# The scheduler takes account of the SBUF port that VectorE and GpSimd share, and the mixers' second weight parts are computed on VectorE

## The chip, the cores and the metric

The kernel runs on one core of a Trainium2 chip. Its engines are TensorE (PE in the profile, its weight loads PEld), VectorE (DVE), ScalarE (ACT), GpSimd (POOL) and SyncE (SP, which here only issues DMAs). The metric is the device time of the whole program in microseconds; lower is better.

## The reference

Four layers over 512 tokens (256 of context, then 256 latent), each with 1024 channels:

```
for l in range(DEPTH):                                  # 4 layers, all in float32
    hg, rw, gt = split(modulate(rms_norm(x)) @ w_in[l]) # 1024 x 6528
    o_hg = hgrn2_branch(hg)     # gated linear recurrence, both directions, 4 heads of 128
    o_rw = rwkv7_branch(rw)     # delta-rule state update, both directions, 8 heads of 64
    m = sigmoid(g_hg) * (o_hg @ proj_a) + sigmoid(g_rw) * (o_rw @ proj_b)
    x = x + gate * rms_norm(m @ w_out)
    x = x + gate2 * rms_norm((silu(gt) * up) @ ffn_w2)  # gt, up = h @ ffn_w1, hidden size 2816
```

Scale, shift and gate of each sub-layer come from a small modulation, silu(c) @ ada_w (1024 x 6144 a layer). In the last layer only the 256 latent tokens are read.

## The kernel before, in words

**Tiles and stages.** Channels lie on the 128 partitions, tokens on the free axis (512 of them). Each layer has two stages. In the *mixers* the input projection feeds four head pairs of RWKV-7 and four heads of HGRN2. In *merge and FFN* come proj_a, proj_b, w_out, the norms and SwiGLU, with the modulation of the next sub-layers computed beside them on VectorE (`ada_pair`: four multiply-adds of 128x512 for each loaded tile `hq` or `PB`).

**Split weights.** Every product is made of three matmuls on rounded numbers. `load_split` loads 128x512 of weights (`wr`), ScalarE rounds them (`wh`, or a place lent by another tile), and another engine subtracts to get the second part (`wl`): `lo = raw - hi`. I call such a subtraction a *second part*. A layer has 270 of them: 102 for the mixers' projection, 16 for proj_a and proj_b, 16 for w_out, 136 for the FFN. Their engine is set by `LO`, with an entry for the mixers and one for the rest in the first three layers, then the same for the last layer: 0 is GpSimd, 1 is either engine, as the scheduler finds them free.

**The mixers' chains.** For an RWKV pair, `rw_solve` inverts triangular matrices with 60 small steps on VectorE (tiles `XS` and `S`), each reading what the one before wrote. `rw_chain` then walks eight chunks: matmuls into `c_ps`, `S0P = S * pcs` on GpSimd, and VectorE's updates of `UV` and `S` that read `S0P`. An HGRN2 head has seven levels, with multiplications `hX`, `hY` on VectorE and running sums `SF`, `PF`, `PB`, `SB` on GpSimd. The projection's matmuls (`p_ps`) fill TensorE between these.

**What sets the order.** All instructions are first written down (`Plan.add`) with a cost from a table (`cost`) and then list-scheduled (`schedule`): each engine takes, of what could start, what the longest chain of work hangs on. The hardware then runs each engine's list in order. The tables `PAR`, `BIAS` and `LOOK` steer that schedule; they are the same before and after.

Of the kernel before, what the change touches and what calls it, by code (L numbers as in the profile page):

```python
# [16 lines left out]
P = 128  # L17
D = 1024
NK = 8
T = 512  # L20
# [41 lines left out]
LO = (1, 0, 1, 1)  # L62
# [9 lines left out]
MAXLOOK = 200  # L72
WINDOW, COLD = 4096 / 1.2, (0.39, 0.87)
# [10 lines left out]
class Node:  # L84
    """One instruction, or several of an engine in a row, with what it waits for."""
# [3 lines left out]
    def __init__(self, engs, calls, preds, costs, load, kind):  # L89
        self.engs, self.calls, self.preds, self.costs, self.load, self.kind = engs, calls, preds, costs, load, kind  # L90


class Plan:
    """Takes down the kernel's instructions, and emits them in the order of a list schedule: each engine runs, of what
    could start, what the longest chain of work hangs on."""
# [10 lines left out]
    def lo(self, i):  # L106
        """The engine of the weights' second parts."""
        return self.any if LO[i] else self.pool

    def tile(self, pool, shape, dt, tag, bufs, name):  # L110
        """A tile; one of a tag takes the place of the one that its tag gave out bufs tiles before."""
# [12 lines left out]
    def region(a):  # L124
        """Partitions and elements that an access pattern spans."""
# [13 lines left out]
    def together(self):  # L139
        """The instructions recorded in this context, all of one engine, stay one after another."""  # L140
        @contextmanager
        def group():
            self.gang = -1
            yield
            self.gang = None
        return group()

    def add(self, engs, name, args, kw):
# [23 lines left out]
        preds.discard(n)  # L172
        b = 4
# [8 lines left out]
        else:  # L182
# [3 lines left out]
            self.nodes.append(Node(engs, [(name, args, kw)], preds, costs, load, self.kind))  # L186
# [8 lines left out]
    @staticmethod  # L195
    def cost(eng, name, out, args, kw):
        """Nanoseconds that an instruction holds its engine."""
# [8 lines left out]
        if eng == "pe":  # L206
# [6 lines left out]
            if args[1].dtype == F32R:  # L213
                return max(n / 2.4, m / 1.2) + 2.5
# [6 lines left out]
        if eng == "vec":  # L221
            if name == "memset":
                return n * 1.05
            two = name in ("tensor_scalar", "tensor_copy") and not psum
# [3 lines left out]
        if name == "tensor_scalar":  # L228
            if ptr:
                return 686.0  # L230
# [10 lines left out]
    def schedule(self):  # L241
# [26 lines left out]
        tail = 1e9  # L268

# [8 lines left out]
        while len(order) < N:  # L278
# [26 lines left out]
            _, i = heapq.heappop(ready[e])  # L305
            x = nodes[i]
            on[i] = e
            c = x.costs[x.engs.index(e)]
# [43 lines left out]
def body(ctx, tc, xT, cc, ada_w, w_in, rw_lo, rw_g2, proj_a, proj_b, w_out, ffn_w1, ffn_w2,  # L352
# [122 lines left out]
    def load_split(src, k0, nk, c0, ncol, place=None):  # L475
        """Weight rows k0*128.. and columns c0.. as its rounded part and the rest."""
# [24 lines left out]
    def psum2(w, src, hi, lo, rg=slice(0, T), tag="s"):  # L501
        """PSUM tile with w^T src for w of zeros and ones, src going in two parts."""
# [7 lines left out]
    def spots(tile):  # L510
        """Places for the split weights of one output tile in [P, 4, T]."""
# [7 lines left out]
    def proj(src, nk, c0, xh, xl, t0, place=None):  # L519
        """PSUM tile with W[:, c0:c0+128]^T x for tokens t0.., with a place for the weights stream by stream."""  # L520
# [24 lines left out]
    def norms(xs, t0, post=None, pre=None):  # L545
        """x += G * rms_norm(y), and then h = rms_norm(x) * A + B per channel and stream, split in two parts."""
# [79 lines left out]
    def ada_put(pm, b, n, ps):  # L626
        """Sums of n blocks of columns from b on, each stream's in 128 / 2 n rows, put channel-major in md."""
# [12 lines left out]
    def ada_first(l, pm):  # L640
        """The first four blocks of 512 columns of silu(c) @ ada_w[l], each in a quarter of the rows."""
# [14 lines left out]
    def ada_pair(l, pm, b):  # L656
        """Blocks b and b + 1, the products summed over the rows of each partition first."""
# [22 lines left out]
    def ada_finish(pm, i):  # L680
        """Scale, shift and gate of sub-layer i // 3 with the norm weights in."""
# [31 lines left out]
    def sigm(o, src, nb, t):  # L713
        """o = sigmoid(src - nb) by exp and ln; t is all of o."""
# [5 lines left out]
    def shifted(ps, j, lmu, t0, tag):  # L720
        """pf = p + mu (shift(p) - p) of projection tile j."""
# [20 lines left out]
    def layer(l, pm, xs, xd, hh, hl):  # L742
# [772 lines left out]
```

## Time and profile before

| | us |
|---|---|
| median of 3 runs | 4484.12 (4477.95 to 4488.85) |
| span of the profiled execution | 4491.0 |
| VectorE busy in it | 3314.2 (74%) |
| TensorE busy in it | 4151.3 (92%) |
| GpSimd busy in it | 2318.9 (52%) |

The profiled execution's span is 6.9 us (0.15%) over the median and 2.2 us over the slowest of the three runs; no work is shown outside the span. Shares of busy time are averages over stages; TensorE's matmuls overlap each other in the records, so its share says little by itself.

### The profile page before, as it was taken

Reading aid. Unit: us, or ns where it says so; the run is one execution under the profiler, and the core shown is the slowest. Engines: PE = TensorE matmul, PEld = TensorE weight load, DVE = VectorE, ACT = ScalarE, POOL = GpSimd, SP = SyncE. Lnnn points to the kernel's source line nnn. Section 1 sums busy time; section 2 is a strip of 40 time slices with the busy share of each in tenths; the row PEclk is TensorE's granted clock in tenths of the full one; section 3 lists DMA queues with packets and bytes.
Section 4 is the critical chain, followed back from the end, with each engine's and each line's share of the span. In section 5 each row is a group of like instructions: output and inputs, shape, how many; then the busy total and the mean of one; then the engine's idle time right before and its main releaser. Section 6 shows DMA issues by size and latency. Waiting matters only on the chain. (4 is left out here: it accounts for less than half of the span.)

```text
span 4491.0 us, 72501 instructions
## 1 busy us (share of the span) xinstructions
PE 4151.3 (92%) x26290; PEld 3248.2 (72%) x26290; DVE 3314.2 (74%) x5772; ACT 2161.3 (48%) x4458; POOL 2318.9 (52%) x2121
## 2 busy tenths in 40 slices
PE   7999998899999999989999999999899989888998
PEld 5676776677777767778777676677777766667888
DVE  5988878977388898676627988876754487887665
ACT  4554653433255565534434554554433354554564
POOL 2464654465445456454654554554555535455542
PEclk8998899999998998899999998899999988887999
DMA  4211127455421111354433211116444421111555
GB/s 151 59 46 36 51 88 227 140 166 158 134 73 57 49 44 46 125 173 125 139 114 122 63 49 41 46 56 205 122 146 124 137 67 43 41 44 39 159 151 162
DMA packets 661415, 451.08 MB, mean 100 GB/s; under 512 B 28224, under 2 KB 584256, under 8 KB 661056
## 3 DMA queue, kind: packets, MB, share of 16 engines
q1 hardware_dynamic: 661056, 446.44, 33.1%
q8 instruction: 207, 3.39, 0.3%
q14 instruction: 152, 1.25, 0.1%
HBM read 416.98 MB, written 29.36 MB: 99 GB/s over the span
## 5 line engine op out<-in xcount | busy, mean ns | idle before, releaser
L341 POOL TENSOR_TENSOR wl<-wr,wh 128x512 fp32r<-128x512 f32 x726 | 1017.5, 1404 | 1034.3 <-ACT wh L341 705.9
L341 PE MATMUL p_ps<-hh,wh 128*128 128x512 f32 (+1 forms) x2784 | 1073.7, 398 | 30.2 <-ACT wh L341 15.8
L341 PE MATMUL p_ps<-hh,wl 128*128 128x512 f32 (+1 forms) x2784 | 1053.1, 397 | 30.9 <-POOL wl L341 21.4
L341 PE MATMUL p_ps<-hl,wh 128*128 128x512 f32 (+1 forms) x2784 | 1060.0, 394 | 0.0
L341 ACT ACTIVATE wh<-wr 128x512 fp32r<-128x512 f32 x986 | 610.0, 621 | 844.3 <-PE p_ps L341 678.8
L341 PEld LDWEIGHTS p_ps<-hh,wl 128*128 128x128 f32 x2784 | 544.5, 198 | 157.8 <-POOL wl L341 46.9
L341 PEld LDWEIGHTS p_ps<-hh,wh 128*128 128x128 f32 x2784 | 541.9, 197 | 145.2 <-ACT wh L341 26.9
L341 PEld LDWEIGHTS p_ps<-hl,wh 128*128 128x128 f32 x2784 | 543.4, 198 | 97.0 <-issue 9.2
L341 POOL TENSOR_SCALAR fn<-fn 128x512 f32<-128x512 f32 (+1 forms) x152 | 230.9, 1519 | 177.4 <-ACT fn L341 168.8
L341 DVE TENSOR_TENSOR fn<-fn,p_ps 128x512 f32<-128x512 f32 (+1 forms) x208 | 127.1, 614 | 219.9 <-ACT fn L341 129.0
L341 POOL TENSOR_SCALAR S0P<-S,pcs 128x64 f32<-128x64 f32 x192 | 156.7, 829 | 222.0 <-DVE S L341 221.2
L341 DVE TENSOR_TENSOR wl<-wr,wh 128x512 fp32r<-128x512 f32 x260 | 186.9, 723 | 101.1 <-ACT wh L341 59.7
L341 DVE TENSOR_TENSOR XS<-XS,S 64x30 f32<-64x30 f32 (+14 forms) x480 | 214.0, 446 | 10.8
L341 ACT ACTIVATE fn<-fn 128x512 f32<-128x512 f32 (+1 forms) x304 | 174.3, 574 | 89.7 <-POOL fn L341 84.9
L341 DVE TENSOR_TENSOR S<-XS 64x30 f32<-64x30 f32 (+14 forms) x480 | 207.3, 432 | 10.8
L341 PE MATMUL s_ps<-XS,X8b 64*64 64x64 f32 (+2 forms) x1024 | 147.2, 298 | 23.2 <-ACT X8a L341 14.5
L341 POOL TENSOR_TENSOR SF<-SF,PF 128x256 f32<-128x256 f32 x112 | 90.9, 812 | 139.0 <-ACT hY L341 138.2
L341 PEld LDWEIGHTS s_ps<-XS,X8b 64*128 64x128 f32 (+1 forms) x1024 | 118.9, 196 | 55.2 <-ACT X8a L341 24.1
L341 PE MATMUL s_ps<-XS,BK 64*64 64x64 f32 (+2 forms) x1024 | 139.2, 275 | 13.3 <-DVE XS L341 12.6
L341 PEld LDWEIGHTS s_ps<-XS,BK 64*128 64x128 f32 (+1 forms) x1024 | 107.9, 175 | 58.9 <-issue 37.1
L341 DVE SCALAR_TENSOR_TENSOR UV<-c_ps,pcs,S0P 64x64 f32<-64x64 f32 x384 | 108.6, 283 | 56.1 <-PE c_ps L341 45.6
L341 PE MATMUL p_ps<-SC,wh 128*128 128x512 f32 (+1 forms) x440 | 143.4, 363 | 2.4 <-ACT SC L341 2.2
(525 smaller groups left out, 9554.7 us busy)
## 6 DMA issues: line engine op xcount, KB each, us to landing
wr<-ffn_w SPq DMA_DIRECT2D x512, 256.0 KB, 3.0
wr<-w_in SPq DMA_DIRECT2D x408, 256.0 KB, 2.9
hq<-ada_w SPq DMA_DIRECT2D x242, 256.0 KB, 2.9
PB<-ada_w SPq DMA_DIRECT2D x110, 256.0 KB, 3.0
wr<-w_out SPq DMA_DIRECT2D x64, 256.0 KB, 3.0
gts<-fn SPq DMA_DIRECT2D x48, 256.0 KB, 3.0
wr<-proj_a SPq DMA_DIRECT2D x32, 256.0 KB, 4.5
wr<-proj_b SPq DMA_DIRECT2D x32, 256.0 KB, 3.8
```

The costliest lines, as they stand in the source:

```text
L341: getattr(self.eng[self.on[i]], name)(*args, **kw)
```

## The change

The scheduler gets a notion of the port: `on_port` says which instructions use it (on GpSimd `tensor_tensor` and `tensor_copy`; on VectorE those that touch SBUF alone and have two tensor inputs, or are `tensor_scalar`, `tensor_copy` or `transpose`). When the first candidate of an engine needs the port and the port is taken for over 100 ns more (`PORT`), the scheduler looks through up to 12 candidates for one that doesn't need it. VectorE pays 88 ns when the quadrant of its output changes. Some costs are new (matmuls of 512 columns 229 ns where 216 stood; `S0P` 440 where 686 stood). And `LO` sends all the mixers' second parts to VectorE.

```diff
-LO = (1, 0, 1, 1)
+LO = (2, 0, 2, 1)
+PORT, OVER = 100.0, 200.0
...
     def lo(self, i):
-        return self.any if LO[i] else self.pool
+        return self.vec if LO[i] == 2 else self.any if LO[i] else self.pool
...
+    def on_port(eng, name, out, args, kw):
+        if eng not in ("vec", "pool"):
+            return False
+        ins = [x for x in (kw.get(k) for k in ("in_", "in0", "in1", "data0", "data1", "data")) if hasattr(x, "space")]
+        ins = ins or [x for x in args[1:] if hasattr(x, "space")]
+        if eng == "pool":
+            return name in ("tensor_tensor", "tensor_copy")
+        if not all(str(x.space).endswith("SB") for x in [out] + ins):
+            return False
+        return len(ins) > 1 or name in ("tensor_scalar", "tensor_copy", "transpose")
...
             if args[1].dtype == F32R:
-                return max(n / 2.4, m / 1.2) + 2.5
+                return max(n / 2.35 + 11.0, m / 1.2 + 2.5)
...
+            if name in ("transpose", "tensor_tensor_scan"):
+                return 67.0 + n * (1.1 if name == "transpose" else 2.08)
...
             if ptr:
-                return 686.0
+                return 440.0
...
-            _, i = heapq.heappop(ready[e])
+            r0, i = heapq.heappop(ready[e])
             x = nodes[i]
+            n = x.engs.index(e)
+            if x.port[n] and port > t + PORT:
+                held = [(r0, i)]
+                while ready[e] and len(held) < 12:
+                    r0, i = heapq.heappop(ready[e])
+                    held.append((r0, i))
+                    y = nodes[i]
+                    if on[i] or y.port[y.engs.index(e)] or t + y.costs[y.engs.index(e)] > port + OVER:
+                        continue
+                    break
+                else:
+                    r0, i = held[0]
...
+            if x.quad is not None and e == "vec":
+                if x.quad != quad:
+                    t += 88.0
+                quad = x.quad
+            if x.port[n]:
+                t = max(t, port)
+                port = t + c
```

Since every cost feeds the schedule, the order differs on all engines. As printed, 241 of the mixers' 408 second parts stand on GpSimd before, and none after; of the other subtractions that either engine may do, 25 more stand on GpSimd after. VectorE has 5772 instructions before and 5988 after, GpSimd 2121 and 1905. In merge and FFN of the first three layers all second parts stay on GpSimd.

Two places, both in layer 1, where pair 0's chain meets pair 1's first steps. On GpSimd before, around the chain's `S0P` (HGRN2's sums are `SF`, `PF`, `PB`, `SB`; `SC<-XS` are copies of the next pair's blocks):

```order
L341 TENSOR_SCALAR S0P_2186<-S_1948,pcs_1971 128x64
L341 TENSOR_SCALAR S0P_2187<-S_1948,pcs_1971 128x64
L341 COPY SC_1944<-XS_1943 64x4x64
L341 TENSOR_TENSOR wl_2228<-wr_2226,wh_2227 128x512
L341 COPY SC_1944<-XS_1943 64x4x64
L341 TENSOR_SCALAR S0P_2190<-S_1948,pcs_1971 128x64
L341 TENSOR_SCALAR S0P_2191<-S_1948,pcs_1971 128x64
L341 TENSOR_TENSOR wl_2269<-wr_2267,wh_2268 128x512
```

and the same place on GpSimd after:

```order
L386 TENSOR_SCALAR S0P_2186<-S_1948,pcs_1971 128x64
L386 TENSOR_SCALAR S0P_2187<-S_1948,pcs_1971 128x64
L386 COPY SC_1944<-XS_1943 64x4x64
L386 TENSOR_TENSOR PB_2026<-PB_2026,SB_1976 128x32x8
L386 TENSOR_TENSOR PF_1975<-PF_1975 128x32x8
L386 COPY SC_1944<-XS_1943 64x4x64
L386 TENSOR_TENSOR SB_1976<-SB_1976 128x32x8
L386 TENSOR_SCALAR S0P_2190<-S_1948,pcs_1971 128x64
L386 TENSOR_SCALAR S0P_2191<-S_1948,pcs_1971 128x64
```

The second parts `wl` are gone from between the chain's steps; three of the running sums of an HGRN2 head stand there. On VectorE before, in the last third of pair 1's solve (its steps are the `XS` and `S` rows):

```order
L341 TENSOR_TENSOR S_1948<-XS_1943 64x150
L341 TENSOR_TENSOR XS_1943<-XS_1943,S_1948 64x25x6
L341 TENSOR_TENSOR S_1948<-XS_1943 64x130
L341 COPY_PREDICATED SS_2091<-hgm_89,g_ps_2139 128x256
L341 TENSOR_TENSOR XS_1943<-XS_1943,S_1948 64x26x5
L341 TENSOR_TENSOR S_1948<-XS_1943 64x108
L341 TENSOR_TENSOR hY_2024<-hY_2024,kf_1977 128x16x16
L341 TENSOR_TENSOR XS_1943<-XS_1943,S_1948 64x27x4
```

and the same steps on VectorE after:

```order
L386 TENSOR_TENSOR S_1948<-XS_1943 64x150
L386 COPY_PREDICATED SS_2091<-hgm_89,g_ps_2148 128x256
L386 TENSOR_TENSOR XS_1943<-XS_1943,S_1948 64x25x6
L386 TENSOR_SCALAR X4c_2209<-s_ps_2233 128x512
L386 TENSOR_TENSOR BK_2235<-X8a_2207,BK_2235 128x512
L386 TENSOR_TENSOR wl_2220<-wr_2218,wh_2219 128x512
L386 TENSOR_TENSOR S_1948<-XS_1943 64x130
L386 TENSOR_TENSOR hY_2024<-hY_2024,kf_1977 128x8x32
L386 TENSOR_TENSOR XS_1943<-XS_1943,S_1948 64x26x5
L386 TENSOR_TENSOR hX_2023<-hX_2023,hq_2013 128x512
L386 TENSOR_TENSOR S_1948<-XS_1943 64x108
```

More foreign work stands between two steps of the solve, second parts among it. Counted over the 16 solves, from the first to the last transpose of each, 63 second parts stand inside before and 239 after; between the first and last `UV` update of the 16 chains 69 and 96.

## Rows read from the trace of the kernel before

**Rows 1.** Busy time in the mixers: layers 1 and 3, sum of all four.

```profile
core 0: us, PE busy (x) PEld busy (x) DVE busy (x) ACT busy (x) POOL busy (x), PEclk, DMA share, GB/s
...
1245.00:1895.00 650.00, 612.06 (x4465) 459.23 (x4464) 540.10 (x1040) 356.16 (x771) 346.04 (x354) 0.91 0.20 61
...
3587.00:4190.00 603.00, 536.92 (x3790) 417.54 (x3789) 495.89 (x972) 319.22 (x733) 320.22 (x355) 0.82 0.17 51
sum 2553.00, PE 2360.53 PEld 1783.82 DVE 2115.45 ACT 1390.08 POOL 1349.85; mean PE 590.13 PEld 445.95 DVE 528.86 ACT 347.52 POOL 337.46
```

**Rows 2.** Busy time in merge and FFN, layers 0 and 1.

```profile
680.00:1245.00 565.00, 512.31 (x2346) 400.74 (x2345) 410.30 (x536) 202.04 (x358) 293.56 (x206) 0.97 0.54 162
1895.00:2415.00 520.00, 497.90 (x2315) 401.92 (x2314) 301.77 (x400) 200.02 (x354) 284.28 (x206) 0.98 0.48 144
```

**Rows 3.** Busy time: layer 1's chains, and layer 0's merge.

```profile
1437.00:1827.00 390.00, 366.48 (x2916) 270.99 (x2915) 333.50 (x659) 212.70 (x484) 219.67 (x246) 0.90 0.15 44
...
720.00:840.00 120.00, 91.98 (x403) 68.27 (x402) 116.72 (x158) 38.38 (x73) 59.80 (x42) 0.91 0.60 180
```

**Rows 4.** Waits in layer 1's chains (1437 to 1827 us): total, times, longest.

```profile
POOL S0P L341 <- DVE S L341: 51.2, 14, 10.8
...
POOL wl L341 <- ACT wh L341: 22.4, 11, 5.0
...
DVE SS L341 <- PE g_ps L341: 17.0, 10, 6.7
```

**Rows 5.** Second parts by engine: least, median and longest duration (ns), first and last start.

```profile
L341 POOL TENSOR_TENSOR wl<-wr,wh x726: 731/1297/3208, 51.0 to 4471.5; 128x512 fp32r<-128x512 f32 x175, 128x256 fp32r<-128x256 f32 x7
...
L341 DVE TENSOR_TENSOR wl<-wr,wh x260: 411/692/1778, 46.6 to 4474.0; 128x512 fp32r<-128x512 f32 x126, 128x256 fp32r<-128x256 f32 x4
```

**Rows 6.** Timeline of GpSimd around 247 us: start, duration, instruction.

```profile
246.25 3.18 POOL L341 TENSOR_SCALAR S0P<-S,pcs 128x64 f32<-128x64 f32 x2
```

**Rows 7.** Timeline of VectorE in the same stretch.

```profile
246.73 0.67 DVE L341 TENSOR_TENSOR wl<-wr,wh 128x512 fp32r<-128x512 f32 x1
247.34 0.33 DVE L341 TENSOR_TENSOR XS<-XS,S 64x184 f32<-64x184 f32 x1
247.60 0.67 DVE L341 TENSOR_TENSOR hX<-hX,hq 128x512 f32<-128x512 f32 x1
248.20 0.35 DVE L341 TENSOR_TENSOR S<-XS 64x198 f32<-64x198 f32 x1
```

**Rows 8.** Timeline of GpSimd around 1484 us.

```profile
1483.87 1.27 POOL L341 TENSOR_TENSOR wl<-wr,wh 128x512 fp32r<-128x512 f32 x1 [4.99 <-ACT wh L341]
```

**Rows 9.** Timeline of VectorE in the same stretch.

```profile
1483.67 0.30 DVE L341 TENSOR_TENSOR S<-XS 64x150 f32<-64x150 f32 x1
1484.01 1.30 DVE L341 TENSOR_TENSOR XS<-XS,S 64x150 f32<-64x150 f32 x1
```

**Rows 10.** Timeline of VectorE: first and last mixer instructions held by a second part.

```profile
34.59 1.24 DVE L341 TENSOR_TENSOR S<-S 128x8 f32<-128x8 f32 x1
35.75 0.23 DVE L341 TENSOR_SCALAR lmu<-vv,shm 128x15 f32<-128x15 f32 x1
35.89 0.15 DVE L341 TENSOR_TENSOR S<-S 128x8 f32<-128x8 f32 x1
...
4136.58 1.47 DVE L341 TENSOR_TENSOR y<-y,bv 128x256 f32<-128x256 f32 x1
```

**Rows 11.** The same, first and last held by GpSimd's other two-input work.

```profile
89.10 0.78 DVE L341 TENSOR_TENSOR wl<-wr,wh 128x512 fp32r<-128x512 f32 x1 [1.06 <-ACT wh L341]
...
4183.07 1.47 DVE L341 TENSOR_TENSOR wl<-wr,wh 128x512 fp32r<-128x512 f32 x2
```

**Rows 12.** `S0P` over the whole program: least, median and longest duration (ns).

```profile
L341 POOL TENSOR_SCALAR S0P<-S,pcs x192: 433/632/2887, 232.3 to 4187.1; 128x64 f32<-128x64 f32 x192
```

**Rows 13.** `S0P` in the page's groups: busy us, mean ns, idle time before.

```profile
L341 POOL TENSOR_SCALAR S0P<-S,pcs 128x64 f32<-128x64 f32 x192 | 156.7, 829 | 222.0 <-DVE S L341 221.2
```

**Rows 14.** Waits in layer 1's merge and FFN (1895 to 2415 us).

```profile
ACT wh L341 <- PE p_ps L341: 163.1, 96, 4.2
...
PEld p_ps L341 <- POOL wl L341: 12.3, 16, 2.3
```

More of the change, by code (lines that the diff above doesn't have):

```diff
@@ L87, with __init__ @@
     head = tail = 0.0
-    def __init__(self, engs, calls, preds, costs, load, kind):
+    def __init__(self, engs, calls, preds, costs, load, kind, port, quad):
         self.engs, self.calls, self.preds, self.costs, self.load, self.kind = engs, calls, preds, costs, load, kind
+        self.port, self.quad = port, quad
 class Plan:
@@ L172, in add @@
         preds.discard(n)
+        r = (out.start_partition(),) if hasattr(out, "start_partition") else (0,)
         b = 4
@@ L185, in add @@
                 load = args[1].ap[0][1] / P * (0.37 if out.start_partition() and out.shape[0] <= C else 1.0)
-            self.nodes.append(Node(engs, [(name, args, kw)], preds, costs, load, self.kind))
+            self.nodes.append(Node(engs, [(name, args, kw)], preds, costs, load, self.kind,
+                                   [self.on_port(e, name, out, args, kw) for e in engs], r[0] // 32 if engs[0] == "vec"
+                                   else None))
         if engs[0] == "pe":
@@ L193, in add @@
             x.tail = m / 1.2 if m == b // (4 * out.ap[0][1]) and m <= C else 1e9
+    @staticmethod
+    def on_port(eng, name, out, args, kw):
[8 more added lines that the diff above has]
+        return len(ins) > 1 or name in ("tensor_scalar", "tensor_copy", "transpose")
     @staticmethod
@@ L268, in schedule @@
         tail = 1e9
+        port, quad = 0.0, 0
         def release(i):
@@ L304, in schedule @@
                     continue
-            _, i = heapq.heappop(ready[e])
+            r0, i = heapq.heappop(ready[e])
             x = nodes[i]
-            on[i] = e
-            c = x.costs[x.engs.index(e)]
+            n = x.engs.index(e)
[10 more added lines that the diff above has]
+                    r0, i = held[0]
+                for h in held:
+                    if h[1] != i:
+                        heapq.heappush(ready[e], h)
+                x = nodes[i]
+                n = x.engs.index(e)
+            on[i] = e
+            c = x.costs[n]
+            if x.quad is not None and e == "vec":
[5 more added lines that the diff above has]
+                port = t + c
             if e == "pe":
```

## The prediction

> **What bounds the kernel now.** I read the busy time by stage first. Merge and FFN of layers 1 and 2 are TensorE's: 498 of 520 us busy at 0.98 of the full clock [rows 2], and the largest wait there is ScalarE's for a free buffer that TensorE gives back, while TensorE's weight loads wait 12.3 us for a second part [rows 14]. The mixers are 2553 of the 4491 us. Their clock is only 0.91, in layer 3 0.82, and VectorE is busy 2115 us of them, 83% [rows 1]. In the stretch in which layer 1's four chains run it is busy 333.5 of 390 us, and its own largest wait there is 17.0 us [rows 3, 4]. So the mixers' middle belongs to VectorE, with TensorE filling in and GpSimd at 56%.
>
> What hides in VectorE's busy time is the second thing to see. At 1484.01 us a solve step takes 1.30 us; its sister before it took 0.30 us, and a larger one elsewhere 0.33 us. GpSimd had begun a second part at 1483.87 us that ran 1.27 us [rows 7 to 9]. The step's end is the second part's end plus 0.17 us: VectorE stood still while the record calls it busy. A 128x8 addition takes 1.24 us under such a second part, and 0.15 us a moment later [rows 10].
>
> I took this over the trace: for each VectorE instruction its duration less the median of those of its form that no GpSimd instruction overlaps, counted where it is over 50 ns and put to the GpSimd instruction that overlaps it longest. In the mixers 176 instructions are held by second parts, 134 us in all, 0.76 us each; the first and the last are in [rows 10]. Another 389 are held by GpSimd's other additions and copies, 148 us in all, first and last in [rows 11].
>
> **The change part by part.**
>
> *The second parts that change engine.* 241 leave GpSimd for VectorE in the mixers. Alone, the median on VectorE is 0.69 us and on GpSimd 1.30 us [rows 5], but VectorE's instructions overlap at their edges: after a 128x512 multiplication begun at 247.60 us the next begins at 248.20 us [rows 7]. So each costs VectorE 0.60 us, together +145 us. 25 other subtractions go the other way, -15 us. With the second parts gone from GpSimd, the 176 holds go too, -134 us. Sum: -4 us, nothing. Bounds: if half of the holds fell into time in which VectorE would have waited anyway, +63 us; if VectorE was held for the full 1.30 us by each of the 241 (more than the method sees, since a hold is hidden where two instructions' records overlap), 145 - 15 - 313 = -183 us. I take -4, which has 176 rows behind it.
>
> At this term the Trainium skill has a rule (SBUF — State Buffer, section "SBUF: two separate sides"): the port pair of VectorE and GpSimd is an exclusive lock for a whole instruction, and whoever comes second is fully blocked. Rows 8 and 9 agree in one direction. By the rule alone each GpSimd second part would hold VectorE for its whole length, and the sum would be the -183 us bound. In the other direction a row differs: GpSimd's pair of `S0P` took 3.18 us while VectorE ran four instructions at full speed in it [rows 6, 7], so a GpSimd `tensor_scalar` that had begun did not block VectorE; it was itself held back. The measurement decides, and it is a reason for the rival on `S0P` below.
>
> *GpSimd's relief.* It loses 241 times 1.30 us and gains 25: some -280 us. That is worth nothing by itself, because GpSimd's waits in the chains are for others (51.2 us `S0P` for VectorE, 22.4 us second parts for ScalarE) [rows 4]; it was not what the chains waited for. The cover that makes it free is VectorE's own work.
>
> *The scheduler that knows the port.* The remaining 148 us of holds are the running sums and copies of GpSimd against VectorE's solve steps and `hY`, `hX`. The new scheduler picks another instruction when the port is taken. It gains between 0 (its times are estimates made before the run) and 148 us. I take a third, -50 us, because many of the held instructions are steps of a solve, where the next is not ready and an evasion must find foreign work. That foreign work is indeed there now: 239 second parts inside the solves where 63 stood, by the order shown. The other side of it is that the chains have less foreign work, since fewer instructions of any kind stand between their first and last update.
>
> *From VectorE's time to the program's.* -4 and -50 are -54 us of VectorE. They count where VectorE is what is waited for; I take its busy share in the mixers, 0.83 [rows 1]: -45 us.
>
> *The corrected costs.* TensorE's 512-column matmuls, the transposes, `S0P` and the quadrant change alter the order everywhere, but no instruction's duration. I cost them at 0. For a bound the nearest rows are two like stages: merge and FFN take 565 us in layer 0 and 520 us in layer 1 [rows 2]. Layer 0's has more modulation in it, so 45 us is too much for an order alone; I allow 20 us either way over the program.
>
> *Merge and FFN.* Nothing moves between engines there in layers 0 to 2. TensorE hides VectorE's holds, except in layer 0's merge, where VectorE is busy 116.7 of 120 us with modulation [rows 3]. By the same method 33 us of these are holds (40 instructions). A third of it would be 11 us; half of that may pass through, -5 us.
>
> *Sum.* -45 - 5 = -50 us on the profiled span of 4491.0 us: 4441 us. That span is 1.0015 times the median of the runs, so 4434 us in the metric; I say 4435.
>
> **The rivals.**
>
> *No change.* VectorE's saving is used up by its new second parts, and TensorE in the mixers is busy 92% [rows 1] and takes what is left. For it: the exchange alone sums to -4 us. Against: that TensorE runs at 0.91 of its clock there, so its share is partly slowness. This gives -9 to +9 us, 4475 to 4493 us.
>
> *Slower: `S0P` is starved.* A chain's step needs VectorE's update, then `S0P` on GpSimd, then the next update. `S0P` takes 0.43 us at best and 0.83 us on average [rows 12, 13]: 192 times 0.40 us, 76 us lost already, because VectorE's two-input instructions in a row hold it back [rows 6, 7]. 241 more such instructions go to VectorE, 27 of them between the chains' updates by the order, and the new scheduler leaves GpSimd's `tensor_scalar` out of its port book and plans `S0P` at 0.44 us. Place: the 16 chains. Price: if the mean goes from 0.83 to 1.2 us, 192 times 0.37 us = 71 us, of which the two directions' pair overlaps in waiting, so 35 to 71 us; with the planner's saving not arriving (the +63 us bound times 0.83 is 52 us at worst, 0 at best) it gives +35 to +75 us. Middle: 4539 us. It decides once `S0P`'s mean is over about 1.1 us, at which 50 us are lost.
>
> *Much faster.* Each second part on GpSimd holds VectorE for its whole 1.30 us (the -183 us bound), or the scheduler removes two thirds of the other holds: -183 or -100 us of VectorE, times 0.83, -85 to -150 us, so 4335 to 4400 us, middle 4370 us. (The first of the two is what the Trainium skill's lock, on the page and section above, would give.) For it: the clock of 0.91 and 0.82 in the mixers [rows 1]. Against: TensorE's own fill of the mixers.
>
> *The change doesn't do what it says.* The assignment does: no second part of the mixers is left on GpSimd. That holds stay as they are is the second term at 0, and is in the no-change case.
>
> **How the numbers follow.** A measurement of this kernel can tell about 0.2%, 9 us, from no change. Likeliest, -15 to -90 us: 0.46. Much faster: 0.10. No change: 0.15. Slower, by `S0P` or by an order that suits the old tables `PAR` and `BIAS` no longer: 0.29. So faster 0.56, same 0.15, slower 0.29. The likeliest case's own range is 4395 to 4470 us. The range that should hold 8 in 10 reaches down to 4380 us (half of the much-faster case is left out) and up to 4525 us (about half of the slower one is).
>
> **What would show it.** Right: in the mixers the holds behind second parts are gone and VectorE's busy time is within 60 us of 2115 us, with each mixer stage some 8 to 15 us shorter; the mean of `hX`, `hY` and of the solve's steps falls; merge and FFN of layers 1 and 2 stay at 520 us. Wrong: `S0P`'s mean over 1 us, solves that last longer than before with chains that start later, VectorE's busy share over 90% in the mixers, or a change that sits in merge and FFN, where I expect none.

## The result and the profile after

The changed kernel takes 4549.27 us (median of 4 runs, 4546.37 to 4557.52), and the kernel before 4486.49 us (median of 4 runs, 4477.95 to 4505.84): a ratio of 1.0122, 95% interval 1.008 to 1.0164. It is slower by 63 us, where 50 us less were forecast. The profiled execution spans 4544.6 us.

Below, a layer's mixers last from its first load of `rw_lo` to its second read of `od`, where the chains end; the rest, up to the next layer, is merge and FFN. By this cut the mixers of before are 645.6, 660.5, 663.2 and 629.0 us (2598), and merge and FFN 555.2, 507.7, 509.5 and 275.3 us (1848). The same by stage after (window, length, busy time of each engine with its instructions, granted clock, DMA); layer 1's mixers and its merge and FFN, then layer 3's mixers:

```profile
1279.60:1969.70 690.10, 631.31 (x4502) 473.04 (x4501) 545.59 (x1101) 369.62 (x791) 280.18 (x308) 0.88 0.21 65
1969.70:2450.50 480.80, 471.74 (x2232) 384.87 (x2231) 286.26 (x375) 188.89 (x331) 268.18 (x195) 0.99 0.48 144
...
3624.80:4242.70 617.90, 538.12 (x3903) 419.60 (x3902) 499.16 (x1061) 326.77 (x748) 243.43 (x299) 0.81 0.18 53
```

All four mixers are 702.2, 690.1, 694.2 and 617.9 us, 2704 in all: 106 us longer. Merge and FFN are 533.1, 480.7, 480.2 and 301.9 us, 1796: 52 us shorter. In layer 1's mixers VectorE is busy 546 us with 50 instructions more than by the same cut before (549 us); the clock there falls from 0.91 to 0.88 [rows 1]. VectorE has no more to do; it waits more. Groups of the page after (busy us, mean ns, idle time before, what ended most of it):

```profile
L386 POOL TENSOR_TENSOR wl<-wr,wh 128x512 fp32r<-128x512 f32 x506 | 692.4, 1372 | 701.5 <-ACT wh L386 445.1
...
L386 DVE TENSOR_TENSOR wl<-wr,wh 128x512 fp32r<-128x512 f32 x480 | 350.2, 733 | 161.9 <-ACT wh L386 141.4
...
L386 POOL TENSOR_SCALAR S0P<-S,pcs 128x64 f32<-128x64 f32 x192 | 146.2, 774 | 282.2 <-DVE S L386 281.2
```

`S0P` did not get slower: 774 ns where it was 829 [rows 13]. By the prediction's method, 3 instructions in the mixers are still held by a second part, 2.6 us in all, where it was 134 us. GpSimd's other additions and copies hold 129 us where it was 148 us.

The 16 solves, each from its first to its last transpose, sum to 1732 us after 1401 us, though a solve's steps became shorter (mean of `XS<-XS,S` 372 ns, 446 before). Waits in layer 1's chains (1475.9 to 1865.9 us after; [rows 4] before; the waits' total, times, longest):

```profile
DVE UV L386 <- PE c_ps L386: 13.0, 11, 2.5
DVE wl L386 <- ACT wh L386: 11.7, 9, 3.0
...
DVE SS L386 <- PE g_ps L386: 8.1, 8, 2.0
```

```profile
POOL S0P L386 <- DVE S L386: 86.4, 12, 21.6
```

GpSimd waits longer for VectorE's `S` than before [rows 4], not because VectorE is fuller. What is new is the length of the holes in TensorE's filling (36 us before, 335 us after, counted as below). In this one (all engines) TensorE is busy 1.61 of 10 us, and its clock falls to the lower of its two levels, 0.50, that is 1.2 GHz:

```profile
1543.00:1563.00 20.00, 19.86 (x103) 13.25 (x101) 18.39 (x40) 15.51 (x33) 15.58 (x15) 1.00 0.24 70
1563.00:1573.00 10.00, 1.61 (x11) 1.14 (x11) 9.14 (x18) 6.44 (x12) 6.51 (x7) 0.77 0.07 26
1573.00:1583.00 10.00, 4.04 (x49) 3.88 (x48) 9.89 (x14) 3.71 (x7) 1.81 (x4) 0.50 0.00 0
1583.00:1593.00 10.00, 8.10 (x144) 7.84 (x141) 9.92 (x13) 1.77 (x3) 0.00 (x0) 0.50 0.24 70
1593.00:1603.00 10.00, 10.00 (x72) 7.73 (x73) 6.89 (x17) 4.07 (x10) 0.87 (x2) 0.50 0.04 12
```

The same stretch, the projection's instructions (those of tile `p_ps`) alone: from 1573 to 1603 us TensorE has none.

```profile
1543.00:1563.00 20.00, 15.50 (x56) 9.77 (x55) 2.77 (x7) 1.29 (x2) 1.00 0.24 70
1563.00:1573.00 10.00, 0.80 (x3) 0.30 (x2) 2.05 (x5) 0.67 (x1) 0.77 0.07 26
1573.00:1583.00 10.00, 0.00 (x0) 0.00 (x0) 0.40 (x1) 0.00 (x0) 0.50 0.00 0
1583.00:1593.00 10.00, 0.00 (x0) 0.00 (x0) 0.00 (x0) 0.00 (x0) 0.50 0.24 70
1593.00:1603.00 10.00, 0.00 (x0) 0.00 (x0) 0.00 (x0) 0.00 (x0) 0.50 0.04 12
```

VectorE's timeline shows what came late: one second part at 1555.68 us, then transposes and products of the next pair, and the next second parts 32 us later. The two that begin at 1589.4 and 1590.0 us (one row, x2), of HGRN2's weights, follow their first parts by 31.0 and 28.2 us. SP's queue, which loads the weights, waits 19.1 us for second parts in one piece.

```profile
1555.68 0.68 DVE L386 TENSOR_TENSOR wl<-wr,wh 128x512 fp32r<-128x512 f32 x1
...
1572.67 1.94 DVE L386 STREAM_TRANSPOSE AR<-XS 32x1024 f32<-32x1024 f32 x1
...
1583.53 1.89 DVE L386 STREAM_TRANSPOSE AR<-XS 32x1024 f32<-32x1024 f32 x1
...
1588.18 0.68 DVE L386 TENSOR_TENSOR wl<-wr,wh 128x512 fp32r<-128x512 f32 x1
...
1589.39 1.28 DVE L386 TENSOR_TENSOR wl<-wr,wh 128x512 fp32r<-128x512 f32 x2
```

```profile
SPq L386 <- DVE wl L386: 23.6, 5, 19.1
```

Two numbers follow this through all runs, both for the mixers of layers 0 to 2. *Holes*: the sum of all stretches over 8 us in which no `p_ps` matmul begins. *Lateness*: the mean time from the end of a first part's rounding (`wh`) to the start of its second part.

### The profile page after: what moved, and what is told of

The parts are those of the page before. It is cut to its first block, busy times and chain, and to the rows that moved or that the text cites. A ratio compares the mean times of both kernels' runs of the same rounds, so it can differ in the third digit from the quotient of the medians.

```text
span 4544.6 us, 72417 instructions
## 1 busy us (share of the span) xinstructions
PE 4179.2 (92%) x26290; PEld 3277.6 (72%) x26290; DVE 3282.0 (72%) x5988; ACT 2168.6 (48%) x4458; POOL 2012.5 (44%) x1905
## 5 line engine op out<-in xcount | busy, mean ns | idle before, releaser
L386 POOL TENSOR_TENSOR wl<-wr,wh 128x512 fp32r<-128x512 f32 x506 | 692.4, 1372 | 701.5 <-ACT wh L386 445.1
L386 DVE TENSOR_TENSOR wl<-wr,wh 128x512 fp32r<-128x512 f32 x480 | 350.2, 733 | 161.9 <-ACT wh L386 141.4
L386 POOL TENSOR_SCALAR fn<-fn 128x512 f32<-128x512 f32 (+1 forms) x152 | 240.6, 1583 | 266.3 <-ACT fn L386 239.0
L386 POOL TENSOR_SCALAR S0P<-S,pcs 128x64 f32<-128x64 f32 x192 | 146.2, 774 | 282.2 <-DVE S L386 281.2
L386 POOL COPY SC<-XS 64x256 f32<-64x256 f32 x128 | 67.5, 527 | 310.1 <-DVE SC L386 295.8
L386 PE MATMUL s_ps<-XS,X8b 64*64 64x64 f32 (+2 forms) x1024 | 160.2, 319 | 33.2 <-DVE XS L386 14.1
L386 DVE TENSOR_TENSOR S<-XS 64x30 f32<-64x30 f32 (+14 forms) x480 | 183.3, 382 | 9.6
L386 DVE TENSOR_TENSOR XS<-XS,S 64x30 f32<-64x30 f32 (+14 forms) x480 | 178.6, 372 | 9.7
```

What stands on the lines that cost most here:

```text
L386: getattr(self.eng[self.on[i]], name)(*args, **kw)
```

## The experiments

Three theories were set against each other. Theory 1: the second parts on VectorE stand inside the solves and hold them. Theory 2: the port rule in the scheduler makes a worse plan, whatever the assignment. Theory 3: any new order costs, since `PAR` and `BIAS` suit the old one. All ratios of the experiments are to the kernel before, run beside them on the same chip; the stages, holes and lateness are those of each kernel's one profiled execution.

| run | ratio (95%) | mixers, merge + FFN (us) | holes (us) | lateness (us) |
|---|---|---|---|---|
| before | 1 | 2598, 1848 | 36 | 1.21 |
| after | 1.0122 (1.008 to 1.0164) | 2704, 1796 | 335 | 5.78 |
| a_lo_back | 1.0361 (1.033 to 1.0392) | 2831, 1799 | 604 | 1.31 |
| b_lo_vec | 1.0138 (1.0107 to 1.0169) | 2597, 1922 | 294 | 3.67 |
| c_costs | 0.9998 (0.9982 to 1.0013) | 2527, 1934 | 109 | 0.88 |
| d_port | 1.0342 (1.0312 to 1.0372) | 2838, 1773 | 656 | 1.70 |
| e_quad | 1.0026 (1.0005 to 1.0046) | 2565, 1901 | 227 | 1.22 |
| f_serial | 1.0353 (1.0323 to 1.0383) | 2844, 1778 | 511 | 1.99 |
| g_skip | 1.0012 (0.9989 to 1.0034) | 2609, 1865 | 54 | 1.34 |
| h_outside | 0.9908 (0.9882 to 0.9934) | 2632, 1782 | 99 | 1.27 |
| i_onesided | 1.0177 (1.0148 to 1.0206) | 2746, 1789 | 307 | 1.36 |
| j_lo_last | 0.9846 (0.9817 to 0.9875) | 2615, 1774 | 91 | 1.29 |
| k_outside_vec | 0.9954 (0.9935 to 0.9973) | 2584, 1844 | 274 | 4.07 |
| n_lo_vec_late | 1.0138 (1.0108 to 1.0168) | 2570, 1944 | 223 | 4.05 |
| p_gate | 1.0070 (1.0044 to 1.0095) | 2592, 1886 | 237 | 2.96 |
| p_prio | 1.0002 (0.9988 to 1.0015) | 2526, 1923 | 141 | 2.90 |
| s_half | 0.9898 (0.9873 to 0.9924) | 2555, 1862 | 155 | 1.45 |
| t_both | 0.9931 (0.9907 to 0.9956) | 2612, 1810 | 180 | 1.67 |
| u_both_last | 0.9930 (0.9904 to 0.9956) | 2610, 1814 | 195 | 1.64 |
| v_mended | 0.9861 (0.9835 to 0.9887) | 2580, 1818 | 208 | 3.75 |

A mixers' stage can be short because projection work was left for after the chains (c_costs: 2527 and 1934, at the same time as before). So the two columns are read together.

### The change taken apart: assignment, costs, port rule

a_lo_back is after with the old assignment; b_lo_vec is before with the new one; c_costs is before with the new costs of the diff alone; d_port has the port rule and the quadrant's penalty alone.

```diff
 a_lo_back, on after
-LO = (2, 0, 2, 1)
+LO = (1, 0, 1, 1)
 b_lo_vec, on before
-LO = (1, 0, 1, 1)
+LO = (2, 0, 2, 1)
-        return self.any if LO[i] else self.pool
+        return self.vec if LO[i] == 2 else self.any if LO[i] else self.pool
 d_port, on a_lo_back
-                return max(n / 2.35 + 11.0, m / 1.2 + 2.5)
+                return max(n / 2.4, m / 1.2) + 2.5
...
-                return 440.0
+                return 686.0
```

> The changed kernel with the old entry for the mixers' second parts (either engine); the new scheduler and its costs stay. Theory 1 (second parts forced onto VectorE stand inside the RWKV solves, 239 instead of 63 by the order, and hold the next solve step back while they wait for ScalarE): with 17 of them left inside the solves the mixers of layers 0 to 2 go back to about 646 to 665 us each, merge and FFN keep the 22 to 29 us a layer that they gained, so the ratio to before is 0.98 to 0.99. Theory 2 (the port rule itself passes over the solve's steps in favour of foreign work): the mixers stay at 690 to 700 us, ratio 1.005 to 1.015. Theory 3 (any order other than the one that the steering tables were made for is worse): ratio 1.005 to 1.02.

> The kernel before with one entry changed: the mixers' second parts all on VectorE, with the old scheduler that knows no port. Theory 1 (second parts on VectorE lengthen the solves): 126 of them stand inside the solves instead of 63, the mixers get 10 to 25 us longer each, ratio 1.01 to 1.02. Theory 2 (the port rule is what costs): the exchange alone is worth nothing, ratio 0.995 to 1.003, since VectorE's extra 145 us are paid by the 134 us of holds that go. Theory 3 (steering tables): ratio 1.005 to 1.02.

> The kernel before with the three corrected costs alone (matmuls of 512 columns, transposes and scans, the multiplication by a pointer scalar on GpSimd). Theories 1 and 2: within 0.5% of before, and the merge and FFN part of the gain, if it comes from the matmul cost, shows as 20 us less in layers 1 and 2. Theory 3 (any new order costs): ratio 1.005 to 1.02.

> The port rule and the quadrant penalty alone: old costs, old entry for the second parts. Theory 1: mixers as before or 5 to 10 us shorter each, ratio 0.98 to 1.0, merge and FFN shorter by 20 us a layer if the port rule is what helped there. Theory 2: mixers 30 us longer each, ratio 1.01 to 1.02. Theory 3: ratio 1.005 to 1.02.

The costs change nothing (0.9998). The port rule alone costs 3.4%, the assignment alone 1.4%, and both together only 1.2%. So Theory 2 is right in kind, but a_lo_back and d_port lie above every range that was written for them, and b_lo_vec's loss is none of the port's. With the second parts free for either engine, the port rule puts 329 (d_port) or 345 (a_lo_back) of the mixers' 408 on GpSimd, where the trace of before has 238; fixed on VectorE they can't go there. Theory 3 falls with c_costs. Theory 1 falls too: in b_lo_vec the 16 solves sum to 1118 us, 283 us less than before, and it is slower all the same. (p_prio below is the reverse: its solves sum to some 275 us more than b_lo_vec's, and it is faster.)

### Which line of the port rule

```diff
 e_quad: d_port without the passing over and the booking
-            if x.port[n] and port > t + PORT:
+            if False and x.port[n] and port > t + PORT:
...
-            if x.port[n]:
-                t = max(t, port)
-                port = t + c
 f_serial: d_port without the passing over and the quadrant
 g_skip: d_port without the quadrant, port known but not waited for
-                t = max(t, port)
-                port = t + c
+                port = max(t, port) + c
 h_outside: d_port, for merge, FFN and modulation only
+            outside = (x.kind is None or x.kind[0] == "A")
-            if x.port[n] and port > t + PORT:
+            if outside and x.port[n] and port > t + PORT:
...
-            if x.port[n]:
+            if outside and x.port[n]:
```

> The kernel before with the 88 ns quadrant penalty alone (no port rule, old costs, old entry for the second parts). If the port rule is what costs 3.4% with either-engine second parts, this stays near before: ratio 0.99 to 1.01. If any new order costs (steering tables), 1.01 to 1.03; but the corrected costs alone came out at 1.000, which speaks against that.

> The booking of the port alone: an instruction on the port starts when the port is free, but nothing is looked for in its place, no quadrant penalty. If the plan's belief that VectorE and GpSimd exclude each other is what makes a bad order (it takes VectorE for fuller than it is, sends second parts to GpSimd and lets it run ahead of TensorE): ratio 1.02 to 1.04, GpSimd computes over 300 of the mixers' second parts, mixers 40 to 60 us longer each. If the passing over of candidates is what costs: ratio 1.00 to 1.01.

> The passing over alone: a candidate on a taken port is replaced by one that needs no port, but no instruction is moved to a later time. If the passing over puts foreign work into the solves: ratio 1.015 to 1.035 with longer solves; if the booking is the cause, ratio 0.99 to 1.01.

> Port rule and quadrant penalty only for instructions outside the mixers' streams (merge, FFN, norms, modulation), old costs, old entry. TensorE's idle time in merge and FFN fell from 22 to 26 us to 8 to 10 us a layer in every run with the port rule so far, and the stage by 22 to 30 us; the mixers keep their order nearly. If that is the port rule's work: merge and FFN 480 to 490 us in layers 1 and 2, mixers 640 to 665 us, ratio 0.98 to 0.99, faster than both kernels. If the shorter merge and FFN was only work that had been done in the longer mixers: ratio 0.997 to 1.005.

The booking (`t = max(t, port)`, `port = t + c`) carries the whole 3.5%. Passing over costs nothing, and the quadrant 0.3%. The loss is all in the mixers: with the rule outside them only, the kernel is 0.9% faster than before (0.9908, at the edge of the 0.98 to 0.99 that was expected).

In f_serial the projection runs out ahead of the chains: its last product, the gates' `gts`, is written 50 us before layer 1's chains end (8 us after that in before). Its end of the mixers, all engines, and then the `p_ps` instructions alone:

```profile
1957.00:1985.00 28.00, 18.99 (x164) 14.34 (x163) 13.99 (x40) 8.67 (x20) 7.61 (x9) 0.67 0.38 127
1985.00:2014.00 29.00, 17.85 (x102) 11.02 (x102) 11.49 (x22) 4.55 (x12) 1.59 (x2) 0.56 0.52 175
```

```profile
1957.00:1985.00 28.00, 1.13 (x4) 0.61 (x4) 0.00 (x0) 0.60 (x1) 0.67 0.38 127
1985.00:2014.00 29.00, 0.00 (x0) 0.00 (x0) 0.00 (x0) 0.00 (x0) 0.56 0.52 175
```

57 us in which the chain's small products run all but alone (4 of the projection's matmuls among them), at a clock of 0.67 and 0.56, with VectorE busy half of the time or less.

Merge and FFN gain what the forecast did not expect. Layer 1's in h_outside, and there TensorE's weight loads' wait for second parts, 11.9 us before by the same cut (12.3 us in [rows 14]):

```profile
1879.30:2365.20 485.90, 477.15 (x2260) 389.39 (x2259) 282.08 (x374) 193.70 (x341) 284.14 (x205) 0.99 0.48 147
```

```profile
PEld p_ps L385 <- POOL wl L385: 3.3, 5, 1.3
```

The booking alone does this: in f_serial the same wait (2015.7 to 2496.8 us) is 1.7 us, and its merge and FFN take 1778 us, while e_quad and g_skip gain nothing there (1901 and 1865 us).

```profile
PEld p_ps L380 <- POOL wl L380: 1.7, 3, 1.2
```

### How long the booking should be

i_onesided lets VectorE wait for GpSimd's bookings, but not GpSimd for VectorE's; s_half books half of each instruction.

```diff
 i_onesided, on f_serial
-                t = max(t, port)
-                port = t + c
+                if e == "vec":
+                    t = max(t, port)
+                else:
+                    port = t + c
 s_half, on f_serial
-                port = t + c
+                port = t + 0.5 * c
```

> f_serial (booking everywhere, 1.035) with the booking in one direction: VectorE waits in the plan for GpSimd's port instructions, GpSimd never for VectorE's. In the trace VectorE's holds behind GpSimd are long (0.76 us behind a second part) and GpSimd's second part is stretched only from 1.30 to 1.49 us. If the mutual exclusion is what made the plan too full and sent second parts to GpSimd: ratio 0.99 to 1.01, with fewer than 290 second parts of the mixers on GpSimd. If any booking in the mixers spoils the order: ratio 1.02 to 1.04.

> f_serial (booking everywhere, 1.035) with each booking for half of the instruction's cost. If the plan's trouble is that it excludes VectorE and GpSimd from each other for longer than the chip does: ratio 0.995 to 1.015, between before and one-sided booking (1.018), with fewer than 290 second parts of the mixers on GpSimd. If any booking at all spoils the mixers' order: 1.02 or more.

3.5% becomes 1.8%, and with half a booking a gain of 1.0%. So the idea of the port isn't what harms; how much is booked decides. Neither run fell where it was expected: 1.0177 lies between i_onesided's two ranges, and s_half is better than the better one of its own. In the trace 313 of the mixers' second parts run on GpSimd in f_serial, 305 in i_onesided, 217 in s_half and 238 in before, so the assignment moves along with the booking, and these three runs don't tell the two apart.

Why a full booking harms is argued and not shown. In the mixers of layers 0 to 2 of before, the instructions that the new book would count are busy 1189 us on VectorE and 673 us on GpSimd, 1862 of 1969 us. But this counts time twice in which one stands held by the other. The records of the two overlap for 471 us, and by the prediction's method, used both ways, VectorE's are held 208 us there and GpSimd's 130 us. By the cost table of before the same instructions book 1383 us, 70% of the stage. So the chip, too, keeps the two apart much of the time, and how a plan that books them in full comes to its loss no run here isolates. Half is one value that was tried, not a measure of how long the chip excludes. (In merge and FFN half a booking does not give the gain: the wait is 12.9 us there, the whole of merge and FFN 1862 us.)

```profile
PEld p_ps L380 <- POOL wl L380: 12.9, 17, 2.3
```

### What the assignment costs

n_lo_vec_late plans every second part as if ScalarE's result came 0.8 us later, so that VectorE meets it ready. p_gate leaves the second parts of the gates' weights (32 in a layer, of `kind` G) free for either engine. p_prio keeps them on VectorE, but without the gates' entry in `BIAS`, which ranks them 477 us behind the others in the first three layers and 53 us in the last.

```diff
 n_lo_vec_late, on b_lo_vec
+        plan.nodes[-1].late = 800.0
...
-end + self.LAG[e][nodes[s].engs[0]]
+end + self.LAG[e][nodes[s].engs[0]] + (nodes[s].late if e == "act" else 0.0)
 p_gate, on b_lo_vec
+        eng = plan.any if plan.kind and plan.kind[0] == "G" else ada["lo"]
-        ada["lo"].tensor_tensor(out=lo, in0=raw,
+        eng.tensor_tensor(out=lo, in0=raw,
 p_prio, on b_lo_vec
+        plan.nodes[-1].late = float(bool(plan.kind) and plan.kind[0] == "G")
...
-        rank = [r + bias_of(BIAS, x.kind) for
+        rank = [r + (0.0 if x.late else bias_of(BIAS, x.kind)) for
```

> b_lo_vec (second parts on VectorE, old scheduler, 1.014) with one edit: the plan takes a second part for ready 0.8 us later after ScalarE's rounding. If the cost of the assignment is that a second part stands at the head of VectorE's queue and waits there for ScalarE (54 us of such waits in b_lo_vec's mixers against 24 us before), the waits fall under 20 us and the ratio to 1.000 to 1.007. If the cost is that second parts now share one engine with the chains and come late for TensorE: ratio 1.012 to 1.025, TensorE's waits for VectorE's second parts as in b_lo_vec (62 us in the mixers, TensorE and its weight loads together) or more.

> b_lo_vec (second parts on VectorE, old scheduler, 1.014) with the gates' second parts, 32 of a layer's 102, free for either engine again. The gates are the projection's filler with by far the lowest rank. If they starve in VectorE's queue, so that TensorE has nothing to fill in: the gates end before or within 15 us of the chains, the matmuls left over after the chains fall from 2030 to 2045 to under 1980, ratio 0.998 to 1.005. If the gates' second parts are not the cause: ratio 1.010 to 1.016 and 2020 or more left over.

> b_lo_vec with the gates' second parts kept on VectorE, but ranked without the streams' bias of -477000. If they starve only because of their rank: left over under 1980, ratio 0.998 to 1.006. If VectorE's time is what is short: they then push into the solves (180 second parts inside, 126 before), the chains end later, ratio 1.012 to 1.025.

VectorE's waits for ScalarE's first parts, 64 us in b_lo_vec's four mixers, became 32 us in n_lo_vec_late (before: 36 us), and the time did not move (1.0138 both): VectorE standing behind an unready second part isn't the cause. The gates' second parts are: freed, they give back half (1.0070, between p_gate's two ranges); ranked as what they feed on the engine that is always full, all of it (1.0002). Lateness by kind agrees, first and second parts matched by the kernel's own list of instructions: the gates' is 1.38 us in before, 6.62 in b_lo_vec and 3.30 in p_prio, that of HGRN2's weights 1.32, 2.90 and 3.29 (in after both are late, 9.71 and 4.22). One expected sign did not come: the projection's matmuls left over after the chains are as many in p_prio as in b_lo_vec (2236 and 2234 `p_ps` matmuls in layer 1's merge and FFN). The gain is in the mixers (2597 to 2526 us). On GpSimd, busy half of the time, something of the lowest rank still finds its turn; on VectorE it stays behind every step of a pair's preparation. In this hole of b_lo_vec (`p_ps` instructions alone; it lasts from 1361.9 to 1383.3 us) the only second parts are two of the gates', at 1378.8 and 1379.8 us, 27 us behind their first parts:

```profile
1342.50:1362.50 20.00, 14.57 (x51) 8.88 (x49) 3.81 (x8) 1.29 (x2) 1.00 0.14 42
1362.50:1372.50 10.00, 0.00 (x0) 0.00 (x0) 1.43 (x2) 0.60 (x1) 0.75 0.01 2
1372.50:1382.50 10.00, 0.00 (x0) 0.00 (x0) 0.00 (x0) 0.00 (x0) 0.50 0.12 34
```

No weight is loaded (DMA share 0.01), nothing fills TensorE, and its clock falls from 1.00 to 0.50. Layer 1's mixers in b_lo_vec and in p_prio:

```profile
1282.50:1936.10 653.60, 611.80 (x4426) 457.88 (x4425) 535.51 (x1087) 354.02 (x765) 259.70 (x298) 0.89 0.19 58
```

```profile
1258.70:1904.30 645.60, 599.45 (x4423) 447.64 (x4423) 539.79 (x1082) 357.59 (x765) 263.46 (x298) 0.91 0.19 57
```

The same number of matmuls, 12 us less TensorE time at the higher clock, 8 us less stage. That the rank is the cause is shown by p_prio's time; that it acts through the holes and the clock is read from the trace (294 to 141 us of holes), and part of the lateness stays (2.90 us).

### Versions put together

k_outside_vec and j_lo_last are h_outside with `LO = (2, 0, 2, 1)` and `LO = (1, 0, 2, 1)` (VectorE in the last layer alone). t_both is h_outside with half a booking inside the mixers; u_both_last is that with `LO = (1, 0, 2, 1)`; v_mended is t_both with all the mixers' second parts on VectorE and p_prio's ranks.

```diff
 t_both, on h_outside
-            if outside and x.port[n]:
+            if x.port[n]:
                 t = max(t, port)
-                port = t + c
+                port = t + (c if outside else 0.5 * c)
```

> h_outside (port rule only outside the mixers, 0.991) with the mixers' second parts all on VectorE. If the assignment and the booking in the mixers are two separate costs, the assignment's +1.4% adds to h_outside: ratio 1.002 to 1.008, chains' ends near 655 us and 20 us of the projection's matmuls left over after them in layers 0 to 2. If the assignment only costs together with the old order of merge and FFN: 0.985 to 0.995.

> h_outside with the second parts of the last layer's mixers alone on VectorE. Layer 3 ran 8 us shorter in b_lo_vec and 11 us shorter in the mixers of the changed kernel, where only half the columns are multiplied: if that is the assignment's work, ratio 0.988 to 0.990, otherwise 0.990 to 0.995.

> The old assignment and costs; the port's booking and passing over as in the change outside the mixers, and in the mixers a booking of half the cost without passing over. If the full booking harms the mixers only by its length, and gains in merge and FFN by what it avoids there, the two gains add: mixers near the 2555 us of the half booking, merge and FFN near the 1782 us of the booking outside, together 4395 to 4430 us, ratio 0.980 to 0.988. If they are one gain seen in two places (the same waits moved about), it stays at 0.990.

> The same, and the last layer's mixers with their second parts on VectorE. With the booking outside alone this assignment gained 0.6%. If the gain is the last layer's own (half columns, little for TensorE to fill with), it comes again: 4370 to 4410 us, 0.974 to 0.983. If the half booking has already taken it (its last layer's mixers are 598 us against 642 us), nothing: as the run without it.

> The change with both found causes mended and its new costs left out: all the mixers' second parts on VectorE, the gates' without their low rank; half booking in the mixers, full booking outside. If the two causes are the whole of the loss, this is faster than before: 4400 to 4450 us, 0.981 to 0.992. If the assignment has a price of its own beyond the gates' rank once the booking is in (VectorE is the mixers' fullest engine), it stays at 1.000 or above, and the change's loss has a third part.

k_outside_vec (0.9954) comes out at the upper edge of its second case, and prices the rule within the change, where all the mixers' second parts stay on VectorE. Outside the mixers the rule gains 1.8% (1.0138 to 0.9954); inside them, with the new costs, which are worth nothing alone, it loses 1.7% (0.9954 to 1.0122). No second part of the mixers can go to GpSimd there, so this loss comes by another way than the assignment's.

v_mended is the change with both causes mended (without its new costs, and without passing over and quadrant in the mixers, which are worth nothing or little alone), and it is 1.4% faster than before, as expected: no third part of the loss shows, and beside t_both (0.9931) the mended assignment gains. Its lateness of 3.75 us and its 208 us of holes say that these two numbers show where after and b_lo_vec lose, and are no measure of a ratio: that lateness and holes make the time is not shown. j_lo_last is as fast (0.9846, better than its range); both beat before and after. But the gains of h_outside (0.9908) and s_half (0.9898) don't add (t_both, 0.9931), and the last layer's assignment, which gained 0.6% on h_outside, gained nothing on t_both (u_both_last). Why is open. So half a per cent between two plans of this kind isn't explained by these runs.

## Why the prediction was wrong

- **The scheduler that knows the port, -50 us: the step that failed.** It was taken to gain between 0 and 148 us; no loss was in its bounds. The new planner removed 19 of the 148 us of GpSimd's other holds, while its booking alone costs 3.5%, some 160 us (f_serial). Within the change it loses 1.7% in the mixers (75 us) and gains 1.8% outside them (k_outside_vec), so that nothing is left of the -50 us, and the exchange's loss decides. The prediction asked which holds an evasion could save, and not what the wait in the plan (`t = max(t, port)`) does to the order of everything else. Which way that takes is open; the runs show that it grows with what is booked.
- **The second parts that change engine, -4 us, nothing.** As VectorE's busy time this was right: by the cut above the sum over the mixers is 2140 us before and 2127 us after, and of 134 us of holds 2.6 are left. As a price it was not: b_lo_vec costs 1.4%, 62 us. The step priced how long the instructions are, and not when they come. In b_lo_vec a second part begins 3.67 us behind its first part, on average, instead of 1.21 us, and a gate's 6.62 instead of 1.38 us; p_prio's rank for the gates takes the whole loss away. That a late one keeps its weight buffers, so that no new weights are loaded and TensorE's filling stops, is read from the holes shown (a DMA share of 0.01; SP's queue waiting 19.1 us). The prediction named VectorE's saving as what counts and TensorE as what "takes what is left"; it did not see that what TensorE takes has to pass through VectorE first. Its slower case did name an order that suits the old `BIAS` no longer, without a price; in the gates' entry this is what happened.
- **GpSimd's relief, worth nothing.** Its busy time in the mixers fell from 1373 to 1058 us, and no run shows a gain from that: this agrees.
- **The corrected costs, 0.** Right: 0.9998.
- **Merge and FFN, -5 us.** Wrong in size: -52 us in after, -66 us in h_outside. Nothing moved between engines there, as said, but the booking puts GpSimd's second parts at other times, and TensorE's weight loads wait for them 3.3 us in layer 1 of h_outside where it was 11.9 us; f_serial, with 1.7 us, shows that the booking does it. The wait is 8.6 of the 22 us by which that stage got shorter.
- **The rival on `S0P`** gave 4539 us, near what was measured, by luck, for a reason that did not happen: the mean of `S0P` fell from 829 to 774 ns, with more of VectorE's two-input work beside it. What that rival had in its second half, solves that last longer with chains that start later, did happen, by the booking.
- At the lock of the Trainium skill (SBUF — State Buffer, section "SBUF: two separate sides") the prediction let the measurement decide, but its row does not show who came first: VectorE's step below began at 246.13 us, before `S0P` at 246.25 us [rows 6], and its next ones followed without a gap. So that row is no case of a GpSimd instruction that came first and did not block. The booking is close to that lock written as a plan: one engine at a time for an instruction's whole length, without GpSimd's `tensor_scalar`. f_serial and s_half say that for planning this kernel the whole length is worse than no lock by 3.5%, and half of it better by 1.0%.

```profile
246.13 0.34 DVE L341 TENSOR_TENSOR S<-XS 64x184 f32<-64x184 f32 x1
```

## What to carry to other kernels

An instruction's price is its length only where its engine is the limit; an instruction that feeds another engine's filling has a due time, and moving it from an idle engine to a full one needs a new rank with it. A scheduler that is told of a shared port can lose by it even where the port is real: try the rule by stage and with a part of the booking (here 1.035 in full, 0.990 with half) before trusting it. And look for holes in the filling (stretches in which the projection's matmuls are missing) rather than at the busy shares: here VectorE's stayed the same and the program lost 1.2%.

## What was not expected of the hardware

In b_lo_vec the granted clock is 1.00, 0.75 and 0.50 in three neighbouring stretches as the projection's matmuls stop (the rows above). In the last of them TensorE is not idle: all its instructions together keep it busy 9.51 of 10 us, and these small products of the next pair run at the lower level.

```profile
1372.50:1382.50 10.00, 9.51 (x33) 6.58 (x33) 8.32 (x19) 2.70 (x8) 0.92 (x2) 0.50 0.12 34
```

GpSimd's `S0P`, which took 3.18 us beside VectorE's row of two-input work in [rows 6, 7], was on average not slower with 241 more such instructions on VectorE.

And GpSimd's `tensor_scalar`, which `on_port` leaves out of its book, does hold VectorE, but not for its whole length. In the trace of before, VectorE's two-input work in SBUF that begins within 0.1 us after a 128x512 GpSimd instruction is held 1.06 us behind a `tensor_tensor` (median of 41) and 0.39 us behind a `tensor_scalar` (median of 13, longest 0.44 us). Here a solve step takes 0.80 us, where one of the same size took 0.35 us at 248.20 us [rows 7]; it ends 0.65 us before the GpSimd instruction does.

```profile
1582.79 1.49 POOL L341 TENSOR_SCALAR hq<-hq 128x512 f32<-128x512 f32 x1 [2.16 <-ACT hq L341]
...
1582.83 0.80 DVE L341 TENSOR_TENSOR XS<-XS,S 64x198 f32<-64x198 f32 x1
```
